# Plain fp32 operands for three groups of products, and the whole top-256 search on ScalarE

## The chip, the cores and the metric

The kernel runs on one core of a Trainium2 chip. The metric is the device time in microseconds (us) of one execution. TensorE multiplies, VectorE and GpSimd (called DVE and POOL in the profile) work element by element, ScalarE (ACT) applies functions, and SyncE (SP) issues nearly all the transfers, in the order in which they stand in its queue.

## The reference, cut to what matters

One transformer block on x (1024 tokens of 1024 numbers, fp32), with a memory of 256 tokens. Three sublayers follow one another, each behind an RMS norm and with a residual sum.

```python
proj = h @ w_in                     # 1024 -> 256+128+64+8+512+768+24
q_d, q_i = c_q @ w_dsa_uq, c_q @ w_idx_q          # 256 -> 8 heads of 64, each
k_d, v_d = split(c_kv @ w_dsa_ukv)                # 128 -> 64 + 64
idx_score = sum_h w_i[h] * relu(q_i[h] @ k_i.T)   # causal
sel = top_k(idx_score, 256)                       # per query
o_dsa = softmax(q_d @ k_d[sel].T) @ v_d[sel]      # 8 heads
o_nsa = g0 * o_cmp + g1 * o_slc + g2 * o_win      # 8 heads, 3 branches, g = sigmoid
x = x + concat(o_dsa, o_nsa) @ w_out
x = x + softmax(norm(h2 @ w_xq) @ k_m.T) @ v_m @ w_xo     # k_m, v_m of the memory: w_xk, w_xv
x = x + square(relu(h3 @ w_ff_in)) @ w_ff_out             # 1024 -> 4096 -> 1024
```

The three branches of `o_nsa` attend to compressed blocks of 32 keys, to all causal keys (with 16 blocks of 64 in 1024 tokens and 16 chosen, every admissible block is chosen), and to a window of 512.

## The kernel before, in words

The 1024 tokens are eight tiles of 128. A large product takes its operands in two parts: `hi`, the value rounded to the type fp32r, and `lo`, the rest, rounded to fp32r too. For each block of 128 of the inner dimension it then runs three matmuls into one PSUM tile: hi with hi, hi with lo, lo with hi. `gemm` (L286) does this for output chunks 256 wide: `load_w` (L251) issues the transfer of 256 KB of weights, two inner blocks, into the ring `wraw`, and `split_w` (L240) makes `whi` (a copy, mostly on ScalarE, L244) and `wlo` (a subtraction on POOL, sometimes on VectorE, L249). Activations are split where they are transposed: `to_T` (L259) transposes with TensorE, and `split_ps` (L234) makes hi on ScalarE and lo on VectorE. `norm_T` (L267) and `norm_T2` (L275) normalise and call it; `xT` (L310) holds the two results.

The stages:

- `project` (L349) makes queries, keys and values out of w_in and three smaller matrices. It runs for `PARTS`, the tiles 0 to 3, then 4 and 5, then 6 and 7; each part loads and splits all weights anew. `compress` (L473) makes the compressed keys and values of a part.
- `attend` (L825) does attention, tile after tile. `index_mask` (L578) makes the index scores of a tile and finds the 256th largest of each row exactly, by a search over bits: 16 steps over the upper halves of the bits on ScalarE (L618 to L620: compare and count, decide, step), then 16 steps over the lower halves on VectorE (L628 to L630). It is interleaved with the softmaxes of the tile before. `scores` (L651) makes two heads' products, minima and exponentials; `inverse` (L679) makes gate/sum out of the sums (the state `gi` holds 1+exp(-g)) on VectorE, and POOL scales by it (L676). `values` (L688) transposes the probabilities, splits them and multiplies; `finish` (L704) adds the two halves of the result and writes 128x128 to DRAM. The compressed branch (`nsa`, L722, with `cmp_scores`, L730) does the like for 64 keys.
- `memory` (L849) makes keys and values of the memory. `between` (L891) does, for two tiles, the product with w_out, the second norm, the memory attention (w_xq, softmax in `consume_q`, w_xo) and the residual sums (`residual_add`, L885). `mlp` (L979) does, for four tiles, eight rounds `f4`: four blocks of 128 of the hidden layer with matmuls 512 wide (ff_in), relu and square on ScalarE (L1011, L1012), split on POOL (L1014, L1015), and then w_ff_out in four chunks 256 wide (ff_out).

The program is written out in one order by generators. `together` (L110) runs attention against one sequence of other work, `fill` (L1079): projection parts 1 and 2, memory, `between` of tiles 0 and 1, of 2 and 3, `mlp` of tiles 0 to 3, `between` of 4 and 5. Each step yields an estimate of its own cost, and `PACES` (L80) says how much of the sequence goes beside how much attention. Attention of tile 4 can't start before its projection, and `between` of a tile not before its attention. Projection part 0 comes first and alone. After the attention, `between` of tiles 6 and 7 is merged with the rest of the sequence, and `mlp` of tiles 4 to 7 ends the program alone.

Of the kernel before, what the change touches and what calls it, by code (L numbers as in the profile page):

```python
# [9 lines left out]
F32 = mybir.dt.float32  # L10
# [12 lines left out]
P = 128  # L23
# [3 lines left out]
PARTS = ((0, 4), (4, 2), (6, 2))  # L27
# [10 lines left out]
    "p2": {"x4": 3, "st": 1, "relu": 2, "wraw": 2, "whi": 4, "wlo": 4, "c8": 4, "c4": 2, "kraw": 3, "pc": 2},  # L38
# [41 lines left out]
PACES = (1.3, 1.3, 1.3, 1.5, 1.5)  # L80
# [86 lines left out]
def build(nc, tc, I, C, out):  # L167
# [91 lines left out]
    def to_T(pool, x_t, hi, lo, nk):  # L259
# [7 lines left out]
    def norm_T(pool, x_t, gb, hi, lo):  # L267
# [5 lines left out]
        to_T(pool, xn, hi, lo, DM // P)  # L273

    def norm_T2(pool, x_t, gb, hi, lo):  # L275

        ss = small(pool, "nss", 1)
        s.activation(hi, x_t.rearrange("p (k c) -> p k c", c=P), AF.Square, accum_out=ss)
        r = rsqrt_of(pool, ss, DM, 1, "n")
        for c in range(0, DM, 512):  # L280
            xn = ring(pool, "relu", [P, 512])
            v.scalar_tensor_tensor(xn, x_t[:, c:c + 512], r[:, 0:1], gb[c // 512], op0=ALU.mult, op1=ALU.mult)  # L282
            k = c // P
            to_T(pool, xn, hi[:, k:k + 4], lo[:, k:k + 4], 4)

    def gemm(pool, xhi, xlo, nk, nt, wsrc, chunks, consume):  # L286
        for ci, parts in enumerate(chunks):
            w = sum(n for _, n in parts)
            gr = []
            for k0 in range(0, nk, KG):  # L290
# [6 lines left out]
                hi, lo = load_w(pool, [P, kn, w], *srcs)  # L297
                gr += [(hi[:, k, :], lo[:, k, :]) for k in range(kn)]
            for t in range(nt):
                pt = pst(TAGS[pool.name][0], [P, w])  # L300
                for k in range(nk):
                    wh, wl = gr[k]
                    xh, xl = xhi(t, k), xlo(t, k)
# [6 lines left out]
    def xT(pool, nt, tag="x"):  # L310
        xh = pool.tile([P, DM // P, nt * P], F32R, tag=tag + "h", name="xh")
        xl = pool.tile([P, DM // P, nt * P], F32R, tag=tag + "l", name="xl")
        return (xh, xl, lambda t, k: xh[:, k, t * P:(t + 1) * P], lambda t, k: xl[:, k, t * P:(t + 1) * P],
                lambda t: (xh[:, :, t * P:(t + 1) * P], xl[:, :, t * P:(t + 1) * P]))
# [34 lines left out]
    def project(pool, part, pe, st):  # L349
        t0, nt = PARTS[part]  # L350
        gb1 = gain(pool, W["norm1_g"])
        xh, xl, xhf, xlf, xt_of = xT(pool, nt)
        for t in range(nt):
            x_t = ring(pool, "x4", [P, DM])
            nc.sync.dma_start(x_t, I["x"][0, (t0 + t) * P:(t0 + t + 1) * P, :])
            norm_T(pool, x_t, gb1, *xt_of(t))
            yield 1.0
        cq = [ring(pool, "c8", [P, nt, 2, P], F32R) for _ in range(2)]
        ckv = [ring(pool, "c4", [P, nt, P], F32R) for _ in range(2)]
# [25 lines left out]
        def consume(ci, t, pt):  # L385
            T = t0 + t
            if ci in (0, 1):
# [8 lines left out]
                dst = [cq[a][:, t, :, :] if ci == 0 else ckv[a][:, t:t + 1, :] for a in range(2)]  # L396
                to_T(pool, raw[:, 1, :], dst[0], dst[1], w // P)
            if ci == 1:
# [6 lines left out]
                v.tensor_scalar(st["gi"][:, T, :], st["gi"][:, T, :], 1.0, None, op0=ALU.add)  # L405
            if ci in (2, 3):
# [18 lines left out]
        def w_in(chunks, first):  # L425
            return gemm(pool, xhf, xlf, DM // P, nt, W["w_in"], chunks,
# [38 lines left out]
        yield from gemm(pool, lambda t, k: ckv[0][:, t, :], lambda t, k: ckv[1][:, t, :], 1, nt,  # L465
                        W["w_dsa_ukv"], [[(0, 128)]], consume_kv)
        yield from alternate(w_in([[(456, 256)], [(712, 256)]], 2), k_prep())
        for k, name in ((0, "w_dsa_uq"), (2, "w_idx_q")):
            yield from gemm(pool, lambda t, k: cq[0][:, t, k, :], lambda t, k: cq[1][:, t, k, :], 2, nt,
# [69 lines left out]
    def q_prep(aw, t, kind, hg):  # L539
# [8 lines left out]
        else:  # L548
# [7 lines left out]
            v.tensor_scalar(ss, ss, 64 * EPS, None, op0=ALU.add)  # L556
# [22 lines left out]
    def index_mask(aw, st, t):  # L579
# [28 lines left out]
        cnt, ok, goal = small(aw, "tkc", 1), small(aw, "tko", 1), small(aw, "tkg", 1)  # L608
        th = small(aw, "tkt", 2)


        over, step, need = small(aw, "tka", 1), small(aw, "tks", 1), small(aw, "tkn", 1)
        v.memset(need, Wd - 2 * TOPK + 1.0)
        v.memset(th[:, 0:1], 0.5 - 32768.0)
        v.memset(th[:, 1:2], 32768.0)
        c = th[:, 0:1]
        for b in range(15, -1, -1):
            s.activation(mask, hi, AF.Sign, bias=c, accum_out=over)  # L618
            s.activation(step, over, AF.Sign, bias=need)
            s.activation(c, step, AF.Identity, scale=-0.5 * (1 << b), bias=c)  # L620
            yield 0.1
        v.tensor_scalar(c, c, -1.0, None, op0=ALU.mult)
        v.tensor_scalar(mask, hi, c, None, op0=ALU.is_gt, op1=ALU.add, accum_out=cnt)
        v.tensor_scalar(goal, cnt, -1.0, TOPK - 0.5, op0=ALU.mult, op1=ALU.add)
        v.scalar_tensor_tensor(lo, hi, c, lo, op0=ALU.is_equal, op1=ALU.mult)
        c = th[:, 1:2]
        for b in range(15, -1, -1):
            v.tensor_scalar(mask, lo, c, None, op0=ALU.is_ge, op1=ALU.add, accum_out=cnt)  # L628
            v.tensor_scalar(ok, cnt, goal[:, 0:1], float(1 << b), op0=ALU.is_ge, op1=ALU.mult)
            v.scalar_tensor_tensor(c, ok, 0.5 * (1 << b) * (1 if b else 0) - (1 << b), c, op0=ALU.add, op1=ALU.add)  # L630
            yield 0.1
        ti = small(aw, "tki", 2, U32)
        tm, tb = small(aw, "tkm", 1, I32), small(aw, "tkb", 1, U32)
        v.tensor_copy(ti, th)
# [16 lines left out]
    def scores(aw, qh, ql, K, kt0, nk, mask, ginv):  # L651
# [22 lines left out]
        rs = inverse(aw, sums, 2, ginv)  # L674
# [456 lines left out]
```

## Time and profile before

| what | value |
|---|---|
| three runs | 2051.06, 2059.2, 2068.51 us, median 2059.2 us |
| the profiled execution | 2051.99 us, span of its core 2050.2 us |
| mean granted clock of TensorE | 0.922 |
| TensorE busy | 1784.2 us, 87% of the span |
| VectorE, ScalarE, POOL busy | 1219.6, 1070.0, 1120.4 us |
| read from and written to DRAM | 176.13 MB, 20.97 MB |

In the profile, a line of a group gives the source line, the engine, the operation, the tile written and the tiles read, the shape, the count, the busy time with the mean of one, and the idle time in front of these instructions with what ended it. TensorE's matmuls overlap (one begins before the one ahead of it has left the array), so the distance from start to start tells the cost of one, not its length. A windows view gives one row for each stretch of time: its length, the busy time of each engine with the number of instructions in brackets, the clock granted to TensorE, the share of the DMA engines and GB/s.

### The profile page before, as it was taken

The page shows a single profiled execution, that of the slowest core. Times are in us where ns is not written, and L with a number is a line of the kernel's source. Part 1 is how long each engine was busy: PE and PEld are TensorE (multiplying, and loading weights), DVE is VectorE, ACT ScalarE, POOL GpSimd, SP SyncE. Part 2 cuts the span into 40 slices and gives each one's busy share as a digit, 9 for nine tenths or more (in the row PEclk, how much of TensorE's full clock was granted, in tenths as well). Part 3 has the DMA queues.
Part 4 walks back from the last instruction along what each step waited for, and adds up shares of the span by engine and source line. Part 5 has one row for each costly group of instructions (what it writes and reads, how often), then busy time and mean ns, then how long its engine had stood idle before and what let it go on. Part 6 is the DMA issues. An engine that isn't in the chain of part 4 may idle for free. (4 is left out here: it accounts for less than half of the span.)

```text
span 2050.2 us, 34110 instructions
## 1 busy us (share of the span) xinstructions
PE 1784.2 (87%) x11702; PEld 1609.6 (79%) x11702; DVE 1219.6 (59%) x3133; ACT 1070.0 (52%) x2542; POOL 1120.4 (55%) x1186
## 2 busy tenths in 40 slices
PE   5978988878687788779998999999877879999999
PEld 5977877767676687669987888888877868888888
DVE  4547686887777877855568665884545432222222
ACT  4446578586367358644674558555445333232322
POOL 2447877667555374437566567566463344444443
PEclk9998789788889899879999999999989889999999
DMA  8235345244413421212222122112574322222222
GB/s 196 69 118 130 86 132 118 68 154 117 120 52 95 143 89 57 85 43 74 73 73 65 57 67 67 62 58 73 170 224 124 122 95 83 93 83 93 84 92 88
DMA packets 219646, 199.34 MB, mean 97 GB/s; under 512 B 46288, under 2 KB 206160, under 8 KB 219472
## 3 DMA queue, kind: packets, MB, share of 16 engines
q1 hardware_dynamic: 211536, 186.67, 30.6%
q0 software_dynamic: 7936, 10.49, 1.9%
q8 instruction: 92, 1.51, 0.3%
q14 instruction: 82, 0.67, 0.1%
HBM read 176.13 MB, written 20.97 MB: 96 GB/s over the span
## 5 line engine op out<-in xcount | busy, mean ns | idle before, releaser
L249 POOL TENSOR_TENSOR wlo<-wraw,whi 128x512 fp32r<-128x512 f32 (+2 forms) x421 | 556.7, 1330 | 406.1 <-ACT whi L244 395.1
L244 ACT ACTIVATE whi<-wraw 128x512 fp32r<-128x512 f32 (+1 forms) x499 | 310.0, 626 | 395.3 <-PE psS L218 175.0
L218 PE MATMUL psD<-whi,xh 128*128 128x256 f32 (+1 forms) x896 | 263.4, 303 | 33.0 <-ACT whi L244 12.6
L218 PE MATMUL psD<-wlo,xh 128*128 128x256 f32 (+1 forms) x896 | 264.4, 298 | 8.5 <-POOL wlo L249 8.4
L218 PE MATMUL psD<-whi,xl 128*128 128x256 f32 (+1 forms) x896 | 261.1, 295 | 7.4 <-DVE xl L900 7.4
L676 POOL TENSOR_SCALAR S<-S,rs 128x128 f32<-128x128 f32 (+7 forms) x192 | 144.4, 765 | 145.7 <-DVE rs L685 75.1
L218 PEld LDWEIGHTS psD<-whi,xh 128*128 128x128 f32 x896 | 179.9, 205 | 43.0 <-ACT whi L244 15.7
L218 PE MATMUL psD<-whi,h 128*128 128x256 f32 x1024 | 203.5, 285 | 9.0 <-POOL h L1014 3.4
L218 PE MATMUL psS<-whi,h 128*128 128x256 f32 x1024 | 192.3, 287 | 14.5 <-POOL h L1014 6.3
L218 PEld LDWEIGHTS psD<-wlo,xh 128*128 128x128 f32 x896 | 182.3, 204 | 13.6 <-POOL wlo L249 12.2
L672 ACT ACTIVATE S<-S,mn 128x128 f32<-128x128 f32 (+7 forms) x192 | 142.9, 745 | 90.6 <-DVE mn L670 86.8
L249 DVE TENSOR_TENSOR wlo<-wraw,whi 128x512 fp32r<-128x512 f32 (+1 forms) x78 | 77.6, 995 | 186.3 <-ACT whi L244 186.1
L218 PEld LDWEIGHTS psD<-whi,xl 128*128 128x128 f32 x896 | 181.5, 203 | 8.5 <-DVE xl L900 8.2
L218 PEld LDWEIGHTS psS<-whi,h 128*128 128x128 f32 x1024 | 162.3, 193 | 19.7 <-POOL h L1014 8.0
L218 PEld LDWEIGHTS psD<-whi,h 128*128 128x128 f32 x1024 | 165.0, 189 | 13.3 <-POOL h L1014 3.6
L236 DVE TENSOR_TENSOR pl<-psPT,ph 128x512 fp32r<-128x512 f32 (+1 forms) x232 | 142.3, 620 | 46.3 <-ACT ph L235 44.8
L235 ACT ACTIVATE ph<-psPT 128x512 fp32r<-128x512 f32 (+1 forms) x232 | 122.0, 540 | 65.9 <-PE psPT L694 60.2
L694 PE MATMUL psPT<-c_ident,S 128*128 128x128 f32 x816 | 139.9, 289 | 9.8 <-POOL S L676 6.2
L218 PE MATMUL psS<-wlo,h 128*128 128x256 f32 x512 | 145.1, 284 | 0.0
L888 DVE TENSOR_TENSOR b<-psS,b 128x256 f32<-128x256 f32 x144 | 60.2, 423 | 141.2 <-PE psS L218 141.2
L218 PE MATMUL psD<-wlo,h 128*128 128x256 f32 x512 | 143.1, 281 | 0.0
L694 PEld LDWEIGHTS psPT<-c_ident,S 128*128 128x128 f32 x816 | 101.5, 148 | 19.7 <-POOL S L676 10.2
(293 smaller groups left out, 4927.2 us busy)
## 6 DMA issues: line engine op xcount, KB each, us to landing
wraw<-in_w_ff_in_dram SPq DMA_DIRECT2D x128, 256.0 KB, 2.7
wraw<-in_w_ff_out_dram SPq DMA_DIRECT2D x128, 256.0 KB, 2.7
wraw<-in_w_in_dram SPq DMA_DIRECT2D x72, 256.0 KB, 2.8
wraw<-in_w_out_dram SPq DMA_DIRECT2D x64, 256.0 KB, 3.2
wraw<-in_w_xq_dram SPq DMA_DIRECT2D x32, 256.0 KB, 2.7
wraw<-in_w_xo_dram SPq DMA_DIRECT2D x32, 256.0 KB, 2.7
x<-in_w_nsa_cmp_dram SPq DMA_DIRECT2D x24, 256.0 KB, 6.1
qin<-q SPq DMA_DIRECT2D x44, 128.0 KB, 2.3
```

Of the source, the lines that this page charges most:

```text
L218: te.matmul(o, a, b, start=start, stop=stop)
L235: s.activation(hi, src, AF.Copy)
L236: v.tensor_tensor(lo, src, hi, op=ALU.subtract)
L244: s.activation(hi, raw, AF.Copy)
L249: (v if l == "v" else g).tensor_tensor(lo, raw, hi, op=ALU.subtract)
L672: s.activation(S, S, AF.Exp, bias=low, scale=-1.0, accum_out=sums[:, hh:hh + 1])
L676: g.tensor_scalar(Ss[hh], Ss[hh], rs[:, hh:hh + 1], 1.0, op0=ALU.mult, op1=ALU.mult)
L694: te.transpose(p2[:, j, hh, :], S[:, (c + j) * P:(c + j + 1) * P], ident)
L888: v.tensor_tensor(dst, pt, dst, op=ALU.add)
```

## The change

1. **Plain fp32 operands.** `project` for parts above 0, `memory`, and in `between` the products with w_out, w_xq and w_xo take weights and activations as they are, fp32, with one matmul for each inner block in place of three. Weights go through `load_whole`, by turns into the rings `whi` and `wlo`, with no split. `to_T` then only copies, ScalarE and VectorE by turns for the two halves of a row. `between` takes the attention's result straight from its tile, untouched. Part 0 of the projection, attention's own products, and the whole MLP keep their splits.
2. **Parts.** `PARTS` becomes (0, 4), (4, 4): the projection of tiles 4 to 7 loads its weights once, and `compress` runs once less.
3. **The search.** Both halves run on ScalarE.
4. **Small steps.** The gate is inverted once in `project`; `scores` takes only the reciprocal of the sums, POOL multiplies by it and by the gate in one instruction; `inverse` is gone. `finish` is one addition of 64x256 and one transfer. One addition in `q_prep` (L556) moves from VectorE to POOL.
5. **ff_out.** The MLP's second product runs in two chunks 512 wide with four weight loads each (one inner block of 512), in place of four chunks 256 wide with two loads each (two inner blocks of 256).
6. **Pace and costs.** `PACES` becomes (1.35, 1.35, 1.35, 1.75, 1.75); a chunk of a plain product yields 4/3 of the cost that the split one yields.

```diff
-PARTS = ((0, 4), (4, 2), (6, 2))
+PARTS = ((0, 4), (4, 4))
-PACES = (1.3, 1.3, 1.3, 1.5, 1.5)
+PACES = (1.35, 1.35, 1.35, 1.75, 1.75)
+    def load_whole(pool, shape, *srcs):
+        wholes["i"] += 1
+        raw = ring(pool, ("whi", "wlo")[wholes["i"] % 2], shape)
+        for dst, src in srcs:
+            nc.sync.dma_start(dst(raw), src)
+        return [raw]
...
-            split_ps(pt, hi[:, c:c + m, :], lo[:, c:c + m, :])
+            if len(xs) == 2:
+                split_ps(pt, xs[0][:, c:c + m, :], xs[1][:, c:c + m, :])
+            elif c % 8 == 0:
+                s.activation(xs[0][:, c:c + m, :], pt, AF.Copy)
+            else:
+                v.tensor_copy(xs[0][:, c:c + m, :], pt)
...
-                hi, lo = load_w(pool, [P, kn, w], *srcs)
+                ws = load_w(pool, [P, kn, w], *srcs) if len(xs) == 2 else load_whole(pool, [P, kn, w], *srcs)
...
                 for k in range(nk):
+                    if len(xs) == 1:
+                        mm(pt, xs[0](t, k), gr[k][0], k == 0, k == nk - 1)
+                        continue
...
-                yield nk * 3 * w / 2400.0
+                yield nk * (5 - len(xs)) * w / 2400.0
...
+                v.reciprocal(st["gi"][:, T, :], st["gi"][:, T, :])
...
-        for b in range(15, -1, -1):
-            v.tensor_scalar(mask, lo, c, None, op0=ALU.is_ge, op1=ALU.add, accum_out=cnt)
-            v.tensor_scalar(ok, cnt, goal[:, 0:1], float(1 << b), op0=ALU.is_ge, op1=ALU.mult)
-            v.scalar_tensor_tensor(c, ok, 0.5 * (1 << b) * (1 if b else 0) - (1 << b), c, op0=ALU.add, op1=ALU.add)
-            yield 0.1
+        for half, src in enumerate((hi, lo)):
+            c, nd = th[:, half:half + 1], need[:, half:half + 1]
...
+            for b in range(15, -1, -1):
+                s.activation(mask, src, AF.Sign, bias=c, accum_out=over)
+                s.activation(step, over, AF.Sign, bias=nd)
+                s.activation(c, step, AF.Identity, scale=-0.5 * (1 << b), bias=c)
+                yield 0.1
...
-        rs = inverse(aw, sums, 2, ginv)
+
+        v.reciprocal(sums, sums)
         for hh in range(2):
-            g.tensor_scalar(Ss[hh], Ss[hh], rs[:, hh:hh + 1], 1.0, op0=ALU.mult, op1=ALU.mult)
+            g.tensor_scalar(Ss[hh], Ss[hh], sums[:, hh:hh + 1], 1.0 if gate is None else gate[:, hh:hh + 1],
+                            op0=ALU.mult, op1=ALU.mult)
...
-            hi, lo = xt_of(t)
-            g.tensor_scalar(hi, o, 1.0, 1.0, op0=ALU.mult, op1=ALU.mult)
-            v.tensor_tensor(lo, o, hi, op=ALU.subtract)
+            o_of.append(o)
...
-            for c in range(4):
+            for c in range(2):
                 gr = []
-                for k0 in range(0, 4, KG):
...
+                for k in range(4):
+                    r0 = (f4 * 4 + k) * P
+                    gr.append(load_w(pool, [P, 512], (lambda r: r, W["w_ff_out"][r0:r0 + P, c * 512:(c + 1) * 512])))
```

More of the change, by code (lines that the diff above doesn't have):

```diff
@@ L351, in project @@
         gb1 = gain(pool, W["norm1_g"])
-        xh, xl, xhf, xlf, xt_of = xT(pool, nt)
+        whole = part > 0
+        _, xf, xt_of = xT(pool, nt, whole)
         for t in range(nt):
@@ L607, in index_mask @@
         v.tensor_tensor(lo.bitcast(I16), bits[:, :, 0], sgn, op=ALU.bitwise_xor)
-        cnt, ok, goal = small(aw, "tkc", 1), small(aw, "tko", 1), small(aw, "tkg", 1)
+        cnt, low = small(aw, "tkc", 1), small(aw, "tkf", 1)
+        over, step, need = small(aw, "tko", 1), small(aw, "tks", 1), small(aw, "tkg", 2)
         th = small(aw, "tkt", 2)
-        over, step, need = small(aw, "tka", 1), small(aw, "tks", 1), small(aw, "tkn", 1)
-        v.memset(need, Wd - 2 * TOPK + 1.0)
-        v.memset(th[:, 0:1], 0.5 - 32768.0)
@@ L625, in index_mask @@
[L625 to L631, printed above, removed]
+        v.memset(need[:, 0:1], Wd - 2 * TOPK + 1.0)
@@ L891, in between @@
     def between(pool, t0, nt, x2s, keep):
-        xh, xl, xhf, xlf, xt_of = xT(pool, nt, "y" if pool.name == "d2" else "x")
+        o_of = []
         for t in range(nt):
```

138 lines of the change are left out of this document (63 added, 75 removed).

## The prediction

> **What bounds the kernel now.** I read the page first, then the windows view cut where the stages end, then windows of the search, then groups of instructions, then the timeline of the tail. The page gives the span; the windows cut it into the projection of tiles 0 to 3 alone (A), attention of tiles 0 to 4 beside projections, memory and two `between` (B), attention of tiles 5 to 7 beside the MLP (B'), two `between` after the attention (C), and the second MLP alone (D). Behind each engine's busy time stands its number of instructions.
>
> ```profile
> span 2050.2 us, 34110 instructions
> PE 1784.2 (87%) x11702; PEld 1609.6 (79%) x11702; DVE 1219.6 (59%) x3133; ACT 1070.0 (52%) x2542; POOL 1120.4 (55%) x1186
> ...
> core 0: us, PE busy (x) PEld busy (x) DVE busy (x) ACT busy (x) POOL busy (x), PEclk, DMA share, GB/s
> 0.00:145.00 145.00, 120.87 (x998) 118.97 (x998) 73.04 (x159) 68.67 (x186) 55.48 (x60) 0.99 0.45 121
> 145.00:860.00 715.00, 574.12 (x3646) 511.18 (x3647) 546.64 (x1567) 461.90 (x1284) 456.78 (x556) 0.85 0.38 106
> 860.00:1450.00 590.00, 551.65 (x3585) 493.38 (x3584) 397.60 (x1020) 335.82 (x710) 348.68 (x338) 0.97 0.21 66
> 1450.00:1660.00 210.00, 165.23 (x1172) 152.81 (x1171) 103.62 (x218) 89.48 (x177) 89.49 (x87) 0.85 0.52 161
> 1660.00:2050.00 390.00, 372.35 (x2307) 333.24 (x2306) 98.75 (x170) 114.13 (x188) 169.99 (x146) 0.99 0.27 86
> ```
>
> The 87% is a mean over unlike stages. In B' and D TensorE is the bound: 551.65 of 590 us and 372.35 of 390, clock 0.97 and 0.99. In B it isn't, by its own work: from the timeline, one 256-wide matmul at full clock takes 0.120 us from start to start, one 512-wide 0.233.
>
> ```profile
> 1800.34 0.28 PE L218 MATMUL psS<-wlo,h 128*128 128x256 f32 x1
> 1800.46 0.40 PE L218 MATMUL psS<-whi,h 128*128 128x256 f32 x2
> ...
> 1806.70 0.40 PE L218 MATMUL psS<-xh,whi 128*128 128x512 f32 x1
> 1806.93 0.40 PE L218 MATMUL psS<-xh,wlo 128*128 128x512 f32 x1
> ```
>
> So B's 3646 matmuls are 438 us of work (at 0.120) in 715 us. What holds it up are chains through the other engines, so most of the gain can only come from B.
>
> Nearly half of B lies beside a search. Windows of its ScalarE half (two of four rows, and their sum), then of its VectorE half:
>
> ```profile
> 293.00:356.00 63.00, 52.00 (x337) 45.45 (x338) 44.70 (x134) 55.05 (x173) 46.23 (x61) 0.89 0.55 131
> ...
> 783.00:836.00 53.00, 42.35 (x279) 37.39 (x278) 36.11 (x117) 50.49 (x137) 28.23 (x36) 0.88 0.29 88
> sum 220.00, PE 171.51 PEld 151.60 DVE 148.54 ACT 198.36 POOL 134.20; mean PE 42.88 PEld 37.90 DVE 37.14 ACT 49.59 POOL 33.55
> ```
>
> ```profile
> 362.00:386.00 24.00, 18.62 (x113) 17.23 (x112) 22.90 (x84) 11.36 (x36) 19.13 (x26) 0.72 0.21 47
> ...
> 840.00:879.00 39.00, 29.97 (x188) 25.84 (x187) 38.35 (x108) 19.64 (x38) 18.86 (x21) 0.81 0.23 70
> sum 135.00, PE 99.69 PEld 87.49 DVE 129.83 ACT 56.34 POOL 78.28; mean PE 24.92 PEld 21.87 DVE 32.46 ACT 14.08 POOL 19.57
> ```
>
> The reader is to see that the engine that searches is the bound there: ScalarE is busy for 198.36 of 220 us (0.90), VectorE for 129.83 of 135. The eight stretches are 355 us and hold 1682 matmuls, 46% of B's. The other 360 us, which I call the gaps, hold 1964 matmuls, 236 us of work: a pace of 0.65. The groups of B say what else its engines do:
>
> ```profile
> L249 POOL TENSOR_TENSOR wlo<-wraw,whi 128x512 fp32r<-128x512 f32 (+1 forms) x146 | 191.3, 1315 | 77.4 <-ACT whi L244 71.6 <-DMA wraw<-in_w_in_dram 3.9 <-PE psS L218 1.2
> L244 ACT ACTIVATE whi<-wraw 128x512 fp32r<-128x512 f32 (+1 forms) x147 | 91.1, 621 | 87.0 <-DMA wraw<-in_w_out_dram 30.6 <-DMA wraw<-in_w_in_dram 27.8 <-PE psD L218 10.5
> L628 DVE TENSOR_SCALAR_CACHE_REDUCE dmask<-tkl,tkt 128x384 bf16<-128x384 uint16 (+3 forms) x57 | 44.7, 785 | 1.4
> L630 DVE SCALAR_TENSOR_TENSOR tkt<-tko,tkt 128x1 f32<-128x1 f32 x56 | 17.8, 318 | 1.2
> L629 DVE TENSOR_SCALAR tko<-tkc,tkg 128x1 f32<-128x1 f32 x56 | 11.6, 208 | 0.7
> L618 ACT ACTIVATE dmask<-tkh,tkt 128x384 bf16<-128x384 uint16 (+3 forms) x64 | 49.3, 770 | 2.0 <-DVE tkl L607 1.4
> L618 ACT ACTIVATION_READ_ACCUMULATOR dmask<-tkh,tkt 128x1 f32 x64 | 12.3, 192 | 0.0
> L619 ACT ACTIVATE tks<-tka,tkn 128x1 f32<-128x1 f32 x64 | 18.5, 289 | 0.5
> L620 ACT ACTIVATE tkt<-tks,tkt 128x1 f32<-128x1 f32 x64 | 18.5, 288 | 0.7
> ```
>
> **The price of a plain fp32 matmul.** The change runs 836 of them, all but four of them 256 or 224 wide (260 in the projection, 64 in memory, 512 in the eight tiles of `between`), for 2508 split ones, which were 301 us at 0.120. Before runs none, so the price is bounded. From below: one pass like the split ones, 0.12. The only plain fp32 work in the trace are transposes of 128 columns,
>
> ```profile
> 1040.38 0.82 PE L694 MATMUL psPT<-c_ident,S 128*128 128x128 f32 x6
> L218 PEld LDWEIGHTS psD<-whi,xh 128*128 128x128 f32 x896 | 179.9, 205 | 43.0 <-ACT whi L244 15.7
> ```
>
> six in 0.82 us, so (0.82 - 0.28)/5 = 0.108 each and 0.22 for 256 columns, but they only move data. From above: four passes that each wait for a weight load of 0.205, 0.82. I take 0.48: a product of two values in two halves has four partial products, of which the kernel makes three at 0.120, and an exact product needs the fourth too. That is nearest to the matmul rows, which are the same operation. TensorE then gets 836 x 0.48 = 401 us for 301, 100 more.
>
> The Trainium skill, "FP8 and Floating Point Precision", section "TensorE Precision Notes", counts four passes for true FP32. By it the price is 0.48 and the change adds 100 us of TensorE work to a kernel that is 87% busy; no run shows it yet.
>
> **The change, part by part.** *A:* part 0 keeps its splits; the gate's reciprocals are four small instructions. 0.
>
> *B, work.* 580 of the 836 lie here: 438 - 580 x 3 x 0.120 + 580 x 0.48 - 64 x 0.11 (one `compress` less) = 500 us of TensorE work. What goes: POOL's 191.3 and ScalarE's 91.1 of weight splits, with the chain transfer, ScalarE, POOL, matmul. A weight tile is then ready when it has landed.
>
> *B, stretches.* The second half of the search adds 64 steps of 0.770 + 0.192 + 0.289 + 0.288 = 1.54 us, 98.5, to ScalarE. In the stretches ScalarE then has 198.36 + 56.34 + 98.5 less its share of the weight splits (91.1 x 355/715 = 45), 308 us; at the 0.90 that it reaches there now, 342 us for 355. VectorE loses 44.7 + 17.8 + 11.6 = 74 and is no bound. TensorE's share, 46% of 500 = 230, fits.
>
> *B, gaps.* 54% of 500 is 270 us of work. At 0.65 now; A, the same projection with nothing beside it, is busy for 0.83, B' for 0.935. Without the split chains, and with instructions that occupy TensorE four times as long, I take 0.85, near A since transfers and norms remain: 318 us for 360. B: 342 + 318 = 660, **-55**. The cover is the weights' prefetch: `load_whole` waits on SP for a free slot, which TensorE frees now; behind it in SP's queue stand attention's reads of its queries. Today SP waits at L254 mostly for POOL (row below), so the wait changes its releaser rather than begins.
>
> ```profile
> SPq L254 <- POOL wlo L249: 953.2, 358, 23.6
> ```
>
> *Small steps in B.* The reciprocal, the POOL multiply, `finish` and L556 take some 35 us of VectorE's 547 away and put 6 on POOL, which has just lost 191; hidden, as VectorE isn't the bound any more (547 - 74 - 35 of 660). They are counted in the 0.85. One set of w_in loads is saved; the DMA share is 0.38, so 0.
>
> *B'.* The search's two halves for the last two tiles:
>
> ```profile
> 1008.00:1059.00 51.00, 50.74 (x328) 46.17 (x328) 25.12 (x73) 49.08 (x115) 34.21 (x35) 1.00 0.22 68
> 1065.00:1103.00 38.00, 35.90 (x228) 31.50 (x229) 36.91 (x101) 15.81 (x33) 16.20 (x15) 1.00 0.23 70
> 1235.00:1292.00 57.00, 55.14 (x353) 48.93 (x352) 31.18 (x86) 52.77 (x120) 38.30 (x40) 1.00 0.24 74
> 1299.00:1341.00 42.00, 38.15 (x211) 31.61 (x211) 40.77 (x108) 17.87 (x37) 21.88 (x24) 1.00 0.20 61
> ```
>
> TensorE starts 6.4 and 6.2 matmuls per us beside ScalarE's half, 6.0 and 5.0 beside VectorE's. At the first pace the second half is 228/6.4 = 35.6 and 211/6.2 = 34 us, together -10. ScalarE would have 49.08 + 15.81 + 16 x 1.54 = 90 of these 95 us (1008 to 1103), 95 of 106 for the other: nearly full, so +5. ff_out: per round 192 x 0.120 = 23.0 becomes 96 x 0.233 = 22.4, eight times, -5. B': **-10**.
>
> *C.* 256 of the plain matmuls: 256 x (0.48 - 0.36) = +31 of work, in a stage where TensorE is idle for 45 of 210 us at a clock of 0.85. Some 20 of it goes into the idle time which the split chain leaves: **+10**, between +31 and -5.
>
> *D.* The eight rounds again give -5. At the start of ff_out TensorE waits for the last hidden block, then for the residual sum to free PSUM:
>
> ```profile
> 1784.18 0.38 PE L218 MATMUL psS<-whi,h 128*128 128x256 f32 x1 [1.06 <-POOL h L1014]
> 1785.54 0.50 PE L218 MATMUL psS<-whi,h 128*128 128x256 f32 x2 [0.62 <-POOL h L1015]
> 1786.44 0.38 PE L218 MATMUL psS<-whi,h 128*128 128x256 f32 x1 [0.40 <-DVE b L888]
> ```
>
> That is 2.1 us a round, 17 in eight. Ahead of it stand 18 matmuls of the first three blocks for two tiles, 18 x 0.120 = 2.2 us of cover, 18 x 0.233 = 4.2 in the new form, just what is missing. I take -10 of the 17. D: **-15**, between 0 and -22; what is late next is the residual sum, twice as wide.
>
> Sum: -55 - 10 + 10 - 15 = -70 of 2050.2. With the 1.8 us outside the span that is 1982, said as **1980**. The profiled execution (2052.0) is 0.35% below the median of 2059.2. About 1% is what a measurement can tell from no change.
>
> **The rivals.**
>
> *Slower: a plain matmul costs clearly more than 0.48.* Each 0.1 us more costs 580 x 0.54 x 0.1/0.85 = 37 us in the gaps and 26 in C, 63 together. The 70 are gone at 0.48 + 0.11 = 0.59. At 0.65 the time is 1980 + 107 = 2087, at 0.82 2193. For it: weight loads of 0.205 are longer than a matmul's 0.120 and hidden only while the next one runs ahead. Against it: they are hidden in all of D. Chance 0.18.
>
> *No change: the gaps keep their idle time.* They are idle 360 - 236 = 124 us now. If that comes from norms, softmaxes in `consume_q` and transfers rather than splits, gaps are 270 + 124 = 394, and the time is 1980 + 76 = 2056. For it: ScalarE's splits themselves waited 30.6 and 27.8 us for transfers, which don't go away. Against it: POOL waited 71.6 us for ScalarE's splits, which do. Chance 0.15.
>
> *The clock stays where it is.* B's 0.85 is a mean of full clock and slower pieces. If the gaps' 270 us of work meet that clock, they are 270/0.85/0.85 = 374, +56: 2036. The dense stages show 0.97 and 0.99, so a busier TensorE should get more. Chance 0.05.
>
> The Trainium skill, "TensorE: Matmul & The Clock Gate", Part 1, says that the clock is halved or full by how busy TensorE has lately been; the rows of B against B' agree, and by it the longer fp32 instructions raise the clock.
>
> *Faster: as dense as B'.* Gaps at 0.935 are 289 (-29), ff_out's stall goes whole and B' gets its 10 from the search without the 5 (-16 with D), C gains 5 (-15): 1920. A price of 0.22 gives about as much, since VectorE's 546.64 - 148.54 - 129.83 = 268 us in the gaps then bound them. Chance 0.20.
>
> **How the numbers follow.** The forecast, 1930 to 2035, has 0.42. With the rivals the range is 1895 to 2100: it leaves out the upper half of the first rival (0.10) and the lower end of the last (0.07). Faster by over 1% are the forecast, the dense case and half of the clock's: 0.42 + 0.20 + 0.02 = 0.64; within 1% the idle gaps and the rest of the clock's, 0.18; slower 0.18.
>
> **What would show it.** Price: the distance of two plain matmuls in the changed kernel's timeline, 0.48; above 0.59 the forecast falls. B: its end near 805 instead of 860, ScalarE over 0.88 busy in the search, TensorE over 0.8 outside it, no POOL row for w_in or w_out. B': TensorE still over 0.93. D: no wait for `h` over 0.3 us at the start of ff_out. The forecast is wrong if B isn't shorter by 25 us at least.

## The result, and the profile after

The changed kernel takes 1861.0 us (median of 4 runs, 1859.0 to 1863.5) where the kernel before takes 2057.0 (2051.1 to 2068.5): a ratio of 0.904, 95% interval 0.900 to 0.908. It is 196 us faster; 72 were forecast, and 1861 lies below the range. The page of the profiled execution comes first, then its windows, cut at the same places of the program as those of before: B ends 3 us ahead of the last matmul of the second `between`, B' 10 us ahead of the first MLP's last, and D begins with the second MLP's first.

```profile
span 1859.0 us, 28028 instructions
PE 1729.4 (93%) x9262; PEld 1467.8 (79%) x9262; DVE 934.9 (50%) x2353; ACT 1077.2 (58%) x2687; POOL 894.7 (48%) x1034
```

```profile
0.00:145.00 145.00, 120.99 (x998) 118.89 (x998) 73.94 (x161) 68.64 (x186) 55.26 (x60) 0.99 0.45 121
145.00:718.00 573.00, 522.58 (x2982) 448.35 (x2983) 377.42 (x1165) 428.92 (x1286) 284.69 (x435) 0.97 0.39 113
718.00:1291.00 573.00, 547.41 (x2832) 458.29 (x2831) 323.48 (x736) 410.99 (x910) 355.56 (x354) 0.97 0.21 64
1291.00:1493.00 202.00, 181.25 (x919) 153.87 (x918) 73.61 (x186) 54.65 (x120) 28.19 (x40) 0.93 0.55 172
1493.00:1859.00 366.00, 357.14 (x1537) 288.43 (x1536) 86.41 (x107) 113.95 (x187) 170.97 (x145) 0.99 0.29 92
```

| stage | before, us | after, us | difference | forecast |
|---|---|---|---|---|
| A | 145 | 145 | 0 | 0 |
| B | 715 | 573 | -142 | -55 |
| B' | 590 | 573 | -17 | -10 |
| C | 210 | 202 | -8 | +10 |
| D | 390 | 366 | -24 | -15 |

By these windows three quarters of the gain are in B. There POOL's busy time fell from 456.78 to 284.69 us and VectorE's from 546.64 to 377.42, and the granted clock rose from 0.85 to 0.97. The windows follow the work beside attention, though, and attention has slid against it: before, the fourth search ended at 879, 19 us behind the end of B; now it ends at 781, 63 us behind. So some of attention has moved from B to B', and the two are best read together: 159 us shorter, where 65 were forecast.

What does a plain product cost? The groups of w_out's products, kept apart by shape, and a row of the timeline:

```profile
L218 PE MATMUL psD<-whi,b 128*128 128x256 f32 x192 | 50.3, 385 | 3.3 <-DMA whi<-in_w_out_dram 2.1 <-DVE b L899 1.0
L218 PE MATMUL psD<-wlo,b 128*128 128x256 f32 x192 | 49.4, 380 | 0.0
...
L218 PE MATMUL psS<-wlo,b 128*128 128x256 f32 x64 | 16.4, 379 | 0.0
...
L218 PE MATMUL psS<-whi,b 128*128 128x256 f32 x64 | 16.2, 380 | 1.8 <-DMA whi<-in_w_out_dram 1.8
```

```profile
419.78 0.38 PE L218 MATMUL psD<-wlo,xh 128*128 128x256 f32 x1
...
420.86 1.03 PE L218 MATMUL psD<-wlo,xh 128*128 128x256 f32 x4
```

Four such records take 1.03 us and one alone 0.38, so they are (1.03 - 0.38)/3 = 0.217 us apart. But the program has 8 tiles x 4 chunks x 8 blocks = 256 products with w_out, and the groups count 192 + 192 + 64 + 64 = 512. The whole program agrees: the 11702 records of before, less 2508 split ones, 1536 in ff_out (half as many, twice as wide) and 64 in `compress`, and with 836 plain products at two records each, are 9266, and the profile has 9262. A plain matmul is two records, and costs 0.43 us, against 0.36 for three split ones. Whoever reads the distance alone gets half the price. In these products TensorE has 836 x (0.43 - 0.36) = 59 us more to do than before, not less.

### The profile page after: what moved, and what is told of

Read it like the earlier page. It is cut to its first block, busy times and chain, and to the rows that moved or that the text cites. A ratio compares the mean times of both kernels' runs of the same rounds, so it can differ in the third digit from the quotient of the medians.

```text
span 1859.0 us, 28028 instructions
## 1 busy us (share of the span) xinstructions
PE 1729.4 (93%) x9262; PEld 1467.8 (79%) x9262; DVE 934.9 (50%) x2353; ACT 1077.2 (58%) x2687; POOL 894.7 (48%) x1034
## 3 DMA queue, kind: packets, MB, share of 16 engines
HBM read 164.69 MB, written 20.97 MB: 100 GB/s over the span
## 5 line engine op out<-in xcount | busy, mean ns | idle before, releaser
L249 POOL TENSOR_TENSOR wlo<-wraw,whi 128x512 fp32r<-128x512 f32 (+1 forms) x230 | 308.2, 1349 | 322.3 <-ACT whi L244 265.0
L244 ACT ACTIVATE whi<-wraw 128x512 fp32r<-128x512 f32 (+2 forms) x289 | 180.9, 628 | 251.8 <-PE psS L218 150.0
L218 PE MATMUL psD<-whi,xh 128*128 128x256 f32 (+1 forms) x704 | 192.7, 357 | 5.8 <-ACT whi L244 3.5
L218 PE MATMUL psD<-wlo,xh 128*128 128x256 f32 (+1 forms) x704 | 192.5, 354 | 0.8 <-DMA wlo<-in_w_in_dram 0.6
L218 PE MATMUL psD<-whi,h 128*128 128x512 f32 x512 | 177.1, 406 | 9.4 <-POOL h L1024 3.7
L218 PE MATMUL psS<-whi,h 128*128 128x512 f32 x512 | 162.0, 392 | 5.1 <-DVE b L899 5.1
L693 POOL TENSOR_SCALAR S<-S,sums,gi 128x640 f32<-128x640 f32 (+7 forms) x128 | 107.4, 850 | 68.2 <-DVE sums L691 59.2
L218 PE MATMUL psS<-K,qh 128*128 128x384 f32 (+3 forms) x288 | 109.2, 383 | 6.6 <-DVE mn L686 2.6
L218 PE MATMUL psD<-xh,wlo 128*128 128x512 f32 x256 | 102.1, 401 | 0.7 <-POOL wlo L249 0.7
L218 PE MATMUL psD<-wlo,h 128*128 128x512 f32 x256 | 102.3, 402 | 0.0
```

The source lines that it names most:

```text
L218: te.matmul(o, a, b, start=start, stop=stop)
L244: s.activation(hi, raw, AF.Copy)
L249: (v if l == "v" else g).tensor_tensor(lo, raw, hi, op=ALU.subtract)
L693: g.tensor_scalar(Ss[hh], Ss[hh], sums[:, hh:hh + 1], 1.0 if gate is None else gate[:, hh:hh + 1], op0=ALU.mult, op1=ALU.mult)
```

## The experiments

All times are medians of a few runs; the kernel before took 2057 to 2061 us beside each of them. Single edits were taken out of the changed kernel, or put alone into the kernel before.

**The price, doubled.** Each plain product is multiplied twice.

```diff
             for t in range(nt):
                 pt = pst(TAGS[pool.name][0], [P, w])
+                for k in range(nk if len(xs) == 1 else 0):
+                    mm(pt, xs[0](t, k), gr[k][0], k == 0, k == nk - 1)
```

> The changed kernel, in which every product with plain fp32 operands is multiplied twice into the same PSUM tile (the second time overwrites the first, so nothing else changes). The trace of the changed kernel shows 0.216 us from start to start for a plain 256-wide matmul; here a product costs 0.43, near the 0.48 that the forecast took. Theory P (the forecast failed on the price alone): 836 x 0.216 = 181 us more work, of which the forecast's slope (63 us for each 0.1 us) puts 136 on the path, 80 in B and 55 in C: about 1997 us. Theory C (the chains through ScalarE and POOL were the whole gain, TensorE's work hardly counts): under 50 us more, at most 1910 us. On C the two differ by place: if C (1301 to 1493 us in the changed kernel) stays within 15 us, TensorE does not bound it.

Measured: 2182 us, 321 more. The expectation (about 1997, or at most 1910) took the price from the distance of records, 0.216, and was off mostly for that reason: the work added is 836 x 0.43 = 361 us. B and C of this kernel:

```profile
145.00:970.00 825.00, 787.12 (x4319) 689.98 (x4320) 422.18 (x1277) 494.38 (x1421) 307.03 (x463) 0.98 0.28 79
...
1503.00:1814.00 311.00, 285.49 (x1406) 247.32 (x1406) 71.23 (x178) 52.09 (x113) 26.61 (x39) 0.95 0.36 112
```

B grew by 252 us for 580 x 0.43 = 250 of work, C by 109 for 110, B' shrank by 40 as attention had more time beside B. In the changed kernel, work added to TensorE is on the path with 321/361 = 0.89 of its length. Theory C falls.

**Half of the change each.** The plain operands with the two parts alone, and then the rest alone (without the new `finish`, for which there was no room).

```diff
-                hi, lo = load_w(pool, [P, kn, w], *srcs)
+                ws = load_w(pool, [P, kn, w], *srcs) if len(xs) == 2 else load_whole(pool, [P, kn, w], *srcs)
```

> The kernel before with the plain fp32 operands and the two projection parts of four tiles, and nothing else of the change. Theory P and theory C both put most of the gain here: 1900 to 1930 us, with 125 to 155 us gone from 2057. Rival S (the search and the small steps carry it): over 1980 us.

Measured: 1966 us, 93 less than before (ratio 0.955, interval 0.953 to 0.956): between the two cases of the expectation. B and B' of this kernel:

```profile
145.00:747.00 602.00, 537.15 (x2876) 457.73 (x2877) 424.56 (x1417) 353.94 (x1040) 241.94 (x373) 0.92 0.37 106
747.00:1369.00 622.00, 580.32 (x3745) 515.25 (x3744) 450.12 (x1155) 371.10 (x795) 344.18 (x349) 0.98 0.20 61
```

B and B' together are 1224 us, 81 less than before, with the lower half of the search still on VectorE.

```diff
-            v.tensor_scalar(mask, lo, c, None, op0=ALU.is_ge, op1=ALU.add, accum_out=cnt)
+                s.activation(mask, src, AF.Sign, bias=c, accum_out=over)
...
-        rs = inverse(aw, sums, 2, ginv)
+        v.reciprocal(sums, sums)
...
-            for c in range(4):
+            for c in range(2):
```

> The kernel before with the rest of the change (search on ScalarE, small steps without the new finish, ff_out 512 wide, the paces) and split operands everywhere. Theory P: ff_out and the search give what the forecast gave them without the plain operands, 25 to 50 us: 2005 to 2030 us. Rival S: under 1960 us. If ScalarE, which keeps its weight splits here, is overfull with the second half of the search, no gain or a loss: 2050 us or more.

Measured: 2032 us, 27 less (0.986, 0.984 to 0.988), just outside the 2005 to 2030 of theory P. 93 and 27 are 120, not 196.

**Plain operands in the MLP too.**

```diff
-                        mm(pt, wh[:, fs], xh[:, k, :], k == 0, False)
-                        mm(pt, wl[:, fs], xh[:, k, :], False, False)
-                        mm(pt, wh[:, fs], xl[:, k, :], False, k == 7)
+                        mm(pt, gr[k][:, fs], xh[:, k, :], k == 0, k == 7)
```

> The changed kernel with plain fp32 operands in both MLPs too. If a plain matmul costs 2 passes for any width (512 wide: 0.43 us, for three of 0.233 = 0.70), each MLP round of 44.8 us becomes 27.6. D, which is bound by TensorE, falls by 8 x 17 = 137 us or somewhat less; B', beside attention, by 50 to 130, as attention's own chains come out: 1595 to 1680 us. If the price grows worse than in proportion with width, or transfers (4 MB a round in 28 us is 150 GB/s) become the bound, over 1720 us.

Measured: 2025 us, 164 more than the changed kernel, where 1595 to 1680 us were expected at two passes a matmul, and over 1720 if the price grew worse than in proportion or transfers became the bound. It was neither of these: the expectation had again taken half the price. This run showed the two records: the second MLP has 256 plain products in ff_in and the trace twice as many, 0.43 us apart each, 0.86 a product against 0.70 for three split ones. Its timeline (one record, then four) and its D:

```profile
1799.47 0.59 PE L218 MATMUL psS<-xh,whi 128*128 128x512 f32 x1
...
1801.61 1.88 PE L218 MATMUL psS<-xh,whi 128*128 128x512 f32 x4
```

```profile
1578.00:2022.00 444.00, 440.85 (x1024) 193.52 (x1022) 44.24 (x64) 39.36 (x65) 0.00 (x0) 1.00 0.24 74
```

512 products at 0.86 are 440 us, and D is 444 us long instead of 366, though POOL has nothing to do in it any more. The other 86 of the 164 us lie beside and behind the first MLP, in B' and C. Where TensorE is the bound, the split is cheaper.

**The search back on VectorE** (lower half, as before):

```diff
+        for b in range(15, -1, -1):
+            v.tensor_scalar(mask, lo, c, None, op0=ALU.is_ge, op1=ALU.add, accum_out=cnt)
+            v.tensor_scalar(ok, cnt, goal[:, 0:1], float(1 << b), op0=ALU.is_ge, op1=ALU.mult)
+            v.scalar_tensor_tensor(c, ok, 0.5 * (1 << b) * (1 if b else 0) - (1 << b), c, op0=ALU.add, op1=ALU.add)
```

> The changed kernel with the lower half of the search back on VectorE. Plain operands alone took 93 us, the rest of the change alone 27, both 196: some 75 us come only from the two together. Theory Q (it is the queue of ScalarE: the longer search pays only where no weight splits stand behind it): 1915 to 1940 us. Theory N (the small steps or the paces carry the 75 us): 1860 to 1885 us.

Measured: 1886 us, 25 more. Theory Q falls, by 29 us.

**The small steps back.**

```diff
-        v.reciprocal(sums, sums)
+        rs = inverse(aw, sums, 2, ginv)
...
-        oc = small(aw, "oc", 256)[0:64].rearrange("p (h q) -> p h q", h=2)
-        s.activation(oc, pv[64:128], AF.Copy)
-        v.tensor_tensor(oc, pv[0:64], oc, op=ALU.add)
+        tmp = small(aw, "qtb", 256, bufs=1)[0:64].rearrange("p (h q) -> p h q", h=2)
+        s.activation(tmp, pv[64:128], AF.Copy)
+        oc = small(aw, "oc", P)
+        for hh in range(2):
+            v.tensor_tensor(oc[hh * 64:hh * 64 + 64], pv[0:64, hh, :], tmp[:, hh, :], op=ALU.add)
```

> The changed kernel with the small steps around the softmaxes as before (two instructions for gate over sums, two additions in finish, the addition of L556 on VectorE). Theory Q: 1865 to 1885 us. Theory N: over 1905 us.

Measured: 1924 us, 63 more: theory N.

**The split's work without split products**, in the chain, and beside it.

```diff
+        s.activation(raw, raw, AF.Copy)
+        g.tensor_scalar(raw, raw, 1.0, 1.0, op0=ALU.mult, op1=ALU.mult)
         return [raw]
```

> The changed kernel with ScalarE and then POOL copying each plain weight tile in place before its matmuls: products stay plain (0.43 us each, as two records of 0.216), but the chain transfer, ScalarE, POOL, matmul is back with its load on both. Chain and load together are what the plain operands removed, so B should lose most of its 144 us: 1950 to 2000 us. If the gain came from elsewhere (fewer transfers, projection in two parts), under 1890 us.

```diff
+        scr = ring(pool, "wraw", shape)
+        s.activation(scr, raw, AF.Copy)
+        g.tensor_tensor(scr, raw, scr, op=ALU.subtract)
         return [raw]
```

> The changed kernel with the same split work on ScalarE and POOL (0.62 and 1.3 us for each plain weight tile), but into a tile that nothing reads: the load without the chain. If ScalarE's and POOL's time is what was freed, it is as slow as the run with the chain in place, within 20 us. If it is the chain, the wait for two engines ahead of each first matmul, it stays under 1890 us.

In B the second one's copies go through one scratch buffer, so ScalarE also waits there for POOL. Measured: 1916 us (+55) and 1941 us (+80), both outside what was expected (1950 to 2000 or under 1890 for the first; within 20 us of the first or under 1890 for the second). POOL's rows for this work, 145 to 780 us, of the first and of the second:

```profile
L267 POOL TENSOR_SCALAR wlo<-wlo 128x512 f32<-128x512 f32 (+2 forms) x57 | 38.2, 669 | 17.6 <-ACT wlo L266 14.1 <-PE psS L218 2.8
L267 POOL TENSOR_SCALAR whi<-whi 128x512 f32<-128x512 f32 (+1 forms) x56 | 35.8, 638 | 59.2 <-ACT whi L266 58.6
```

```profile
L268 POOL TENSOR_TENSOR wraw<-wlo,wraw 128x512 f32<-128x512 f32 (+2 forms) x57 | 75.7, 1327 | 8.4 <-ACT wraw L267 5.8 <-DMA whi<-in_w_out_dram 1.7 <-DMA whi<-in_w_xo_dram 0.7
L268 POOL TENSOR_TENSOR wraw<-whi,wraw 128x512 f32<-128x512 f32 (+1 forms) x56 | 72.6, 1296 | 40.1 <-ACT wraw L267 38.7 <-DMA wlo<-in_w_xq_dram 1.3
```

The second has no engine between the landing and the matmul and is the slower one. What differs in its disfavour is POOL's load, 148 us against 74, and the one buffer. So the load is dear without the chain. How little TensorE itself waits for a split is told by its waits in B of the kernel before:

```profile
PE psD L218 <- POOL wlo L249: 8.4, 13, 1.2
PE psD L218 <- ACT whi L244: 5.3, 8, 1.1
```

That is 13.7 us in 715. In the run with the chain the like wait is 0.4 us, 145 to 780 us, and in the run with the load alone there is none. So the matmuls' own wait for two engines isn't what most of the gain is made of; a chain without its load wasn't tried, and 55 and 80 us are well below the 151 that plain operands and parts turn out to be worth (below).

**Which small step?** The old `finish` alone; the old `finish` with a buffer of its own for its copy; the old gate alone; and the new `finish` in the kernel before.

> The changed kernel with the old finish only: its copy goes through the buffer qtb, of which there is one and which the query preparation uses too, and two additions follow. The old small steps together cost 64 us. Theory F (finish carries them, because attention's last step and the next query preparation wait for each other over qtb): 1900 to 1925 us. Theory G (the gate over the sums carries them, as POOL waited for it): under 1875 us.

```diff
-        tmp = small(aw, "qtb", 256, bufs=1)[0:64].rearrange("p (h q) -> p h q", h=2)
+        tmp = small(aw, "fin", 256, bufs=1)[0:64].rearrange("p (h q) -> p h q", h=2)
```

> The changed kernel with the old finish, two additions into a 128x128 tile, but its copy in a buffer of its own. If the shared buffer is what costs in the old finish: 1860 to 1875 us. If the additional instruction and the transfer's form cost: as slow as the run with the old finish, 1900 to 1925 us.

> The changed kernel with the old gate over the sums (maximum times gate, then reciprocal, on VectorE, before POOL scales). Theory F: 1862 to 1880 us. Theory G: 1895 to 1925 us.

> The kernel before with the new finish alone (its buffer single, since there is no room for two). If finish carries the small steps and does so without the other parts of the change: 1995 to 2025 us. If it pays only where the split chains are gone: over 2040 us.

Measured: 1916 (+55), 1875 (+14), 1867 (+6, within what the runs can tell) and 2048 (-11; 0.995, 0.993 to 0.997). Each was in a case of its expectation. Theory F holds: `finish` carries the small steps, and 41 of its 55 us are the buffer. `qtb` exists once; the copy of `finish` goes into it, and the next query preparation writes it at L581 and reads it at L584. Two groups of the query preparation, 145 to 1300 us: with the old `finish`, with its own buffer, and before.

```profile
L584 POOL TENSOR_TENSOR qd<-qta,qtb 128x256 f32<-128x256 f32 x43 | 39.2, 912 | 48.2 <-DVE qtb L581 41.9 <-DVE cms L229 3.6 <-PE psPV L218 1.6
...
L574 ACT ACTIVATE qta<-qin 128x256 f32<-128x256 f32 x32 | 13.2, 414 | 34.0 <-DMA qin<-q 29.9 <-POOL qd L584 2.6 <-DVE isc L618 0.8
```

```profile
L584 POOL TENSOR_TENSOR qd<-qta,qtb 128x256 f32<-128x256 f32 x44 | 37.6, 855 | 49.8 <-PE psPT L590 49.6
...
L574 ACT ACTIVATE qta<-qin 128x256 f32<-128x256 f32 x32 | 13.2, 414 | 9.7 <-DVE qd L583 4.5 <-POOL qd L584 4.2 <-DMA qin<-q 0.7
```

```profile
L563 POOL TENSOR_TENSOR qd<-qta,qtb 128x256 f32<-128x256 f32 x41 | 35.8, 874 | 24.7 <-DVE qtb L560 15.4 <-PE psS L218 3.4 <-DVE rs L682 2.3
...
L553 ACT ACTIVATE qta<-qin 128x256 f32<-128x256 f32 x30 | 12.3, 410 | 24.5 <-DMA qin<-q 19.1 <-DVE qd L562 3.7 <-DVE isc L597 0.8
```

With the shared buffer POOL waits 41.9 us for the write of `qtb`, and ScalarE 29.9 for the queries' transfer; with its own buffer the first wait is gone from the row and the second is 0.7. POOL is idle about as long, but now until TensorE's transposes of the group before give `qd` free: it seems to be ahead of its work and no longer behind. The loss appears far from its place: attention ends later, and the last `between`, which needs its last tile, with it. The rows of `finish`'s transfers give the start of the first and of the last, in the changed kernel, with the old `finish`, with its own buffer, and before.

```profile
L717 SPq DMA_DIRECT2D o<-oc x64: 574/587/1067, 185.8 to 1330.0; - x64
L719 SPq DMA_DIRECT2D o<-oc x64: 319/338/1292, 185.0 to 1395.5; - x64
L719 SPq DMA_DIRECT2D o<-oc x64: 319/328/1106, 187.2 to 1342.3; - x64
L710 SPq DMA_DIRECT2D o<-oc x64: 319/338/1428, 184.9 to 1472.6; - x64
```

The last one starts 65 us later with the old `finish` and 12 us later with its own buffer, for 55 and 14 us in the whole. C with the old `finish`, 257 us where it is 202:

```profile
1292.00:1549.00 257.00, 222.26 (x1114) 186.18 (x1113) 111.05 (x287) 82.06 (x176) 47.08 (x60) 0.88 0.44 137
```

Before, both waits were there too (15.4 and 19.1), but there the new `finish` alone gave only 11. Probably something else was later there; no run names it.

**All but the plain operands and the parts**, in the kernel before, now with the new `finish`:

> The kernel before with all of the change but the plain operands and the two parts: search on ScalarE, all small steps with the new finish (its buffer single), ff_out 512 wide, paces. Without the new finish it was 2032. If the gains add up, finish takes another 11 as in the kernel before, or 55 as in the changed one: 2021 or 1977 us. The distance to the changed kernel, 1861, is then what plain operands and parts are worth among the rest: 116 to 160, against 93 alone.

Measured: 2012 us (0.977, 0.974 to 0.979), nearer the 2021 of gains that add up than the 1977. Plain operands and parts are worth 151 us among the rest, 93 alone; the rest 105 beside them, 48 alone. The new `finish` is worth 20 here (2032 to 2012).

**More work in the kernel before:**

```diff
+                for k in range(nk if pool.name != "p1" else 0):
+                    mm(pt, xhi(t, k), gr[k][0], k == 0, k == nk - 1)
                 for k in range(nk):
                     wh, wl = gr[k]
```

> The kernel before with one more hi-with-hi matmul for each of the 836 inner blocks that the change makes plain, overwritten by the three that follow: 836 x 0.120 = 100 us more TensorE work, nothing else. If TensorE's work is on the path there as it is in the changed kernel (321 us for 361, 0.89): 2147 us. The forecast's slope gives 75: 2132 us. If B of the kernel before is held by the other engines and by its slow clock (0.85), under 2100 us, and the clock in B goes up.

Measured: 2128 us, 68 more for 100 of work. B:

```profile
145.00:909.00 764.00, 628.36 (x4240) 569.68 (x4241) 542.55 (x1597) 467.57 (x1290) 461.42 (x559) 0.87 0.36 99
```

49 more for 580 x 0.12 = 70, at a clock of 0.87 instead of 0.85. Work added to TensorE was on the path with 0.68 of its length. The expectation's split (0.89, or under 0.4) met neither end; the forecast's 0.75 was near.

**The plain operands with three parts:**

```diff
-PARTS = ((0, 4), (4, 4))
+PARTS = ((0, 4), (4, 2), (6, 2))
```

> The kernel before with the plain operands alone, and its three projection parts kept. Plain operands with two parts were 1966. The two parts save one set of projection weights (24 of 256 KB), half a compress and some norms' waits: if that counts, 1975 to 1995 us; if plain operands are all of the 93 us, within 8 us of 1966.

Measured: 1985 us, as expected, so joining the parts is worth 20 of the 93.

**Three tries around the changed kernel:** two buffers for `qtb` and one for `oc`; split operands in the last `between`; the old paces.

```diff
-        oc = small(aw, "oc", 256)[0:64].rearrange("p (h q) -> p h q", h=2)
+        oc = small(aw, "oc", 256, bufs=1)[0:64].rearrange("p (h q) -> p h q", h=2)
...
-        tb = small(aw, "qtb", 256, bufs=1).rearrange("p (h d) -> p h d", d=64)
+        tb = small(aw, "qtb", 256, bufs=2).rearrange("p (h d) -> p h d", d=64)
```

> The changed kernel with two buffers for qtb and one for finish's oc, in the same room: a try to go on in the direction of the run with finish's own buffer. If query preparations of following groups still wait for each other over qtb: 1845 to 1857 us. If oc's single buffer, which the transfer holds, costs as much: within 8 us of 1861, or slower.

```diff
+            if pool.name == "d2":
+                if t == 0:
+                    _, of, ot_of = xT(pool, nt)
+                hi, lo = ot_of(t)
+                g.tensor_scalar(hi, o, 1.0, 1.0, op0=ALU.mult, op1=ALU.mult)
+                v.tensor_tensor(lo, o, hi, op=ALU.subtract)
...
-        _, xf, xt_of = xT(pool, nt, True)
+        _, xf, xt_of = xT(pool, nt, pool.name != "d2")
```

> The changed kernel with split operands (three matmuls, 0.36 us) in the last between only, that of tiles 6 and 7, where ScalarE and POOL are nearly idle. TensorE's work there falls by 64 x 2 x (0.43 - 0.36) = 9 us. If the splits stay hidden behind products that last longer than they, 1850 to 1858 us; if the chain through ScalarE and POOL is on the path there as it is in B, 1865 to 1885 us.

> The changed kernel with the old paces. Undone one at a time, finish is worth 55 us, the search 25 and the gate 6; together with ff_out that is already what the rest of the change is worth beside plain operands (105). So the paces should be worth nothing that can be told: 1853 to 1870 us. If they decide how far attention gets ahead of the last between, 1875 us or more.

Measured: 1864, 1868 and 1862 us. None is faster than 1861: a second buffer for `qtb`, paid for with one of `oc`, gains nothing, the splits in the last `between` don't give back the 9 us of work, and the paces are worth nothing that can be told.

## Why the prediction was wrong

- **The small steps: the step that failed.** The forecast called them "hidden, as VectorE isn't the bound any more" and counted them at nothing of their own, within the 0.85 of the gaps. It weighed `finish` by the VectorE time that it takes away. Its worth is in a wait: 55 us, 41 of them for one buffer that two steps used. With the old `finish` the changed kernel takes 1916, which lies inside the range. Rows that pointed at the wait stood in the trace of before (15.4 us for `qtb`, 19.1 for `qin`), though not how much it would be worth, and the whole diff names the buffer in a line that it removes.
- **B's sum: the work beside the searches, the second step that failed.** The forecast let the searches bound their stretches and gave TensorE there its old share of the matmuls: 46% of the work, 230 us in 342, a pace of 0.67, against 0.85 in the gaps. B's part of the searches now (to 718) and its gaps:

```profile
sum 299.00, PE 272.01 PEld 233.91 DVE 183.49 ACT 265.99 POOL 144.40; mean PE 68.00 PEld 58.48 DVE 45.87 ACT 66.50 POOL 36.10
sum 274.00, PE 250.57 PEld 214.44 DVE 193.93 ACT 162.92 POOL 140.28; mean PE 62.64 PEld 53.61 DVE 48.48 ACT 40.73 POOL 35.07
```

  By an estimate from their records, at 0.216 us for one of a plain product and 0.120 for any other, the first hold 245 us of work and the second 223: a pace of 0.82 in both. The gaps came out nearly as forecast; beside the searches TensorE did much more, and the other work was through before the fourth search. That isn't the work of `finish` alone: with plain operands and parts and nothing else, B and B' were already 81 us shorter, and 65 was the forecast of the whole change for these two stages. Which of the freed engines let TensorE run on there stays open.
- **The parts: 0 forecast for the loads that are saved, 20 measured.** The DMA share of 0.38 was the reason for the 0. Both runs of this pair take the projection's weights plain, so no splits of them are among the 20. What goes is 11 MB of reads (176.13 to 164.69 MB) and half of `compress`, 68 matmul records; which of the two counts wasn't separated.
- **The price: right, and a little high.** 0.43 for the 0.48 taken; at the forecast's 63 us for each 0.1 that is an estimate of 32 us. The transposes' 0.22 as an end was misleading, another operation with another price. The Trainium skill, "FP8 and Floating Point Precision", section "TensorE Precision Notes", counts four passes; the trace shows two records and no passes, and 0.43 is 3.6 times the 0.120 of a split matmul.
- **The slope: about right.** 0.75 of the work on the path was forecast; for added work, 0.68 before and 0.89 after were measured.
- **The search: right in size.** 18 us were forecast (13 in B, 10 less 5 in B'), 25 measured by taking it back. Its four stretches in B and at its edge, first and last row and the sum:

```profile
276.00:366.00 90.00, 81.28 (x449) 69.85 (x447) 56.48 (x163) 77.94 (x265) 53.77 (x77) 0.94 0.28 84
...
673.00:781.00 108.00, 87.37 (x456) 72.73 (x454) 61.57 (x150) 93.56 (x231) 48.75 (x55) 0.87 0.19 55
sum 362.00, PE 319.44 PEld 271.67 DVE 212.55 ACT 316.86 POOL 172.40; mean PE 79.86 PEld 67.92 DVE 53.14 ACT 79.21 POOL 43.10
```

  ScalarE is busy for 316.86 of 362 us, 0.875, where 308 of 342 was forecast. The 362 include the few us between the two halves, which the forecast's 355 and 342 leave out; from its first step to its last the four searches took 372 before (293 to 386, 431 to 527, 604 to 691, 783 to 879), so they are 10 us shorter.
- **C: wrong in sign.** -8 for +10, outside the -5 to +31 named. TensorE is busy for longer there, as forecast (181.25 us, 165.23 before), but its idle time fell from 45 to 21 us. How much of C hangs on the end of attention is told by the old `finish`: attention then ends 103 us into C, not 39, and C is 257 us long.
- **D: right in kind.** -24 for -15, just past the -22 named as its end. The wait for `h` at the start of ff_out is gone, and as forecast the residual sum is late next:

```profile
1612.80 0.50 PE L218 MATMUL psS<-whi,h 128*128 128x512 f32 x1 [0.56 <-DVE b L899]
```

- **The clock: only its bad side was priced.** The forecast gave a chance to a clock that stays at 0.85 and no term of its own to one that rises. It rose to 0.97. The Trainium skill, "TensorE: Matmul & The Clock Gate", Part 1, ties the clock to how busy TensorE has lately been; the windows of B agree (0.85 before, 0.87 with 70 us more work, 0.97 after, 0.98 with doubled products). How much of the gain is the clock's own wasn't separated.

From 1980, the price takes 32, `finish` 55, the parts 20, the search's rest 7 and D's rest 9: 1857, against 1861. That is a sum of single edits, `finish` and the search taken out of the changed kernel and the parts out of the plain operands alone; since the edits don't add (93 and 48 alone, 196 together), its closing is partly luck and proves no single entry in another order; the price in it is an estimate. It goes by edits and the reading of B above goes by stages, so the two aren't to be added. 196 - 93 - 48 = 55 us come only from both halves together. `finish` explains some 35 of them: it is worth 55 beside plain operands and 20 without them, the rest of the change being there both times. The other 20 are open.

Of the rivals, the dense case came nearest (1920), though by another mechanism: the gaps stayed at 0.82, not 0.935. The high price fell with 0.43, and the gaps that keep their idle time with that 0.82.

## What to carry to other kernels

Take a plain fp32 product for a split one where the engines that split are late, and not where TensorE is the bound: here such an edit gave 75 us in the first case (plain operands alone in the kernel before, 2061 to 1985) and cost 164 in the second (the MLP). Price a small step by what its buffers tie together, not by the busy time of its engine: look in the diff for a buffer that changes its users, and in the groups for waits at its writer. And when several edits relieve different chains in one stage, a sum of their single effects can be too low: here 93 and 48 against 196.

## What had not been expected of the hardware

In these traces a plain fp32 matmul appears as two records of matmul and weight load each: 2 x 0.217 us for 256 columns, 2 x 0.43 for 512. The count of records against the count in the program tells it; the distance alone halves the price.
